# Sixty-six stores issued by GpSimd's queue instead of the sync engine's, in a hybrid attention and mLSTM step

## The chip, the cores and the metric

The kernel runs on one core of one Trainium2 chip, as one launch. The time is the device time of that core in microseconds (us). Five engines work side by side, each with an instruction queue of its own that it executes in order: PE (TensorE, matrix products; PEld is its weight load), DVE (VectorE), ACT (ScalarE), POOL (GpSimd) and SP (the sync engine, which here only issues DMAs). A DMA is issued by an instruction in the queue of one engine and is then carried out by the DMA engines; whoever needs its data waits for its semaphore. In the profile, "SPq", "ACTq" and "POOLq" are the queues, L729 is line 729 of the kernel, and a tile's name stands without its number.

## The reference, cut to what matters

One layer of a diffusion backbone, for 128 context tokens and 1024 latent tokens, all float32. Every matrix product is as wide as the model (1024) or the feed-forward part (2816).

```python
def trunk_layer(x, mods, ..., rope, ctx_kv, init_f, init_b):
    sh1, sc1, g1, sh2, sc2, g2 = mods            # silu(cond) @ w_ada + b_ada, six vectors
    h = rmsnorm(x, norm1_w) * (1 + sc1) + sh1
    aq, ak, av, mq, mk, mv, mo, mg = jnp.split(h @ w_in, SPLIT_POINTS, axis=-1)
    aq, ak = rmsnorm(aq, q_norm_w), rmsnorm(ak, k_norm_w)      # per head, 64 wide; then rotary
    attn_o = attention(aq, keys, vals)           # 8 query heads on 2 key/value heads
    hm, st_f, st_b = mlstm_bidir(heads(mq), heads(mk) * (MLSTM_DK ** -0.5), heads(mv),
                                 gates, init_f, init_b)        # 4 heads, two directions, chunks of 128
    hm = rmsnorm(hm, mlstm_norm_w) * sigmoid(mo)
    mix = jnp.concatenate([attn_o, hm], axis=-1) @ w_out
    x = x + g1 * mix
    h2 = rmsnorm(x, norm2_w) * (1 + sc2) + sh2
    x = x + g2 * swiglu(h2, w_gu, w_down)
    return x, ak, av, st_f, st_b
```

Returned are the normed outputs of both token groups and, of the context tokens, the keys and values, and the end states C, n and m of both scans of each head.

## The kernel before, in words

The 1152 tokens are nine blocks of 128 rows (block 0 is the context), grouped in three chunks of three blocks. float32 products are made of three PE passes on a rounded high part and the rest (`whi`, `wlo` of a weight, `hi` and `lo` parts of the data), the mLSTM's input products of scaled float16 pairs (`ipair`).

The stages, in order of time:

1. To about 135 us: the conditioning vectors from `w_ada`, the normed and turned tokens, and the projections of keys, values and gates. `k_work` (L688) norms and rotates the keys and stores the context's keys and values (L694, L695).
2. 115 to 195 us: `gate_work` (L535) computes the gates of all scans; it stores `new_state_m` (L617) and copies a three-part bfloat16 split of its maxima into a tile of another layout, SBUF to SBUF, with six DMAs (L648). Beside it `evac_q` (L716) norms and rotates the queries in groups of one or two blocks: POOL multiplies (L668, L685), DVE adds (L686), and each block goes to the DRAM tile `q_d` (L729), from which ACT's queue loads it again as `qr` (L999) for the attention.
3. 193 to 530 us: for each of four heads `head_project` (L743) makes queries, keys, values and output gates of nine blocks and updates the state of both directions block by block (`update`, L779: POOL forms `wv` in L783, PE multiplies in L785, DVE and ACT add to `cs`, L792 and L796). The end states of each head go to the outputs (L800, L801: two directions, two stores each). `head_mlstm` (L825) then reads the scans out, norms the result (L893, POOL) and stores a head's columns of `hm` into the DRAM tiles `hm_d` (L895), one store for each chunk of three blocks. `hm` has one buffer, so the next head's first write waits for these stores. Woven in are the first chunk's attention (`attention`, L991) and, at the end, the rest of the conditioning (`ada_rest`, L417), which takes its bias rows from DRAM (L448) and puts finished rows into the DRAM tile `g_d` (L454), and the first chunk's attention output (`attn_out_first`, L1205), which stores the sum as `x1a_d` (L1247).
4. 530 to 660 us: `prefill` (L1149) adds the mLSTM half of the output projection for all nine blocks: it loads `hm_d` (L1158) and `x1a_d` (L1163), and for the blocks of later chunks loads `x` (L1193), adds, and stores into `x1_d` (L1197).
5. 660 to 1590 us: the feed-forward part, chunk by chunk, in groups of four or five blocks of 128 hidden columns: `gate_up` (L1316), `down` (L1339), and `finish` (L1351), which norms the previous chunk and stores it to `y` (L1363). The last chunk ends in `down_last` (L1366), whose stores stand on ACT's and SP's queues (L1402, L1403).

Weights come through `load_piece` (L139, its DMA L151) and `ada_rest`'s L423 on SP, as do nearly all loads and the attention's transposing DMAs of the softmax's high and low parts (L1041, L1042). `dma` is `nc.sync.dma_start`.

What sets the order: the code yields between units of work and `weave` and `beside` mix these streams by given shares (`weave(head_project(0, sts[0]), beside((att, 0.1),), 96, 96)`). The tile framework then places each instruction in its engine's queue by a planner that plays the program through with durations of its own (`schedule_with_timeline_sim=True`); `hot(n)` raises the priority of a stretch. So an edit to one queue can also shift instructions on the other engines. The framework adds the semaphores: a store waits for its data, the next writer of a buffer for the store.

Of the kernel before, what the change touches and what calls it, by code (L numbers as in the profile page):

```python
# [19 lines left out]
P = 128  # L20
# [8 lines left out]
NH = 4  # L29
# [4 lines left out]
CB = 3  # L34
# [11 lines left out]
def hybrid_step(ctx: ExitStack, tc: tile.TileContext, I: dict, O: dict):  # L46
    nc = tc.nc
# [2 lines left out]
    dve = nc.vector  # L50
    pool = nc.gpsimd
    dma = nc.sync.dma_start
    uid = [0]

    def hot(n):
# [361 lines left out]
    def ada_rest(ns, silp, new_a4, new_part, new_row, early=2):  # L417


        def rows_of(n, j, q, half):  # L420
            a4 = new_a4()
            lo = n * D + j * 512 + q * 256
            dma(a4, w_ada[half * 512 : half * 512 + 512, lo : lo + 256].rearrange("(k p) n -> p k n", p=P))  # L423
            return a4

        units = [(n, j, q, half) for n in ns for j in range(2) for q in range(2) for half in range(2)]
        ahead = [rows_of(*u) for u in units[:early]]
        for u, (n, j, q, half) in enumerate(units):
            if u + early < len(units):
                ahead.append(rows_of(*units[u + early]))  # L430
            yield
            a4 = ahead.pop(0)
            if q == 0 and half == 0:
                ps = bank()
            for k in range(4):
                strip_products(ps[:, q * 256 : (q + 1) * 256], 4 * half + k, silp, a4[:, k, :])
            yield
            if q == 0 or half == 0:
                continue
            part = new_part()  # L440
            nc.scalar.copy(part, ps)
            yield
            if n in (3, 4):
                cols_from_strips(shift2 if n == 3 else scale2, n, j, part, bank)
                continue
            lo = n * D + j * 512
            row = new_row()
            dma(row, I["b_ada"][0:1, lo : lo + 512].to_broadcast([2, 512]))  # L448
            pr = bank()
            mm(pr[0:2, :], strip_sel, part, start=True, stop=True)  # L450
            dve.tensor_tensor(out=row, in0=pr[0:2, :], in1=row, op=ALU.add)
            if n == 5:
                dve.tensor_scalar(out=row, in0=row, scalar1=0.5, scalar2=None, op0=ALU.mult)
            dma(g_d[0 if n == 2 else 1, :, j * 512 : (j + 1) * 512], row)  # L454
        yield

    es_r = ExitStack()
# [77 lines left out]
    def gate_work(mlp):  # L535
# [57 lines left out]
        sm = g1("sm", rows=1)  # L593
# [3 lines left out]
        def blk(t, d, lo, hi):  # L597
            return t[:, d * 64 + 4 * lo : d * 64 + 4 * hi]
# [15 lines left out]
        dve.tensor_copy(blk(Mp, 1, 8, 9), m0[:, 4:8])  # L614
        dve.tensor_copy(blk(Mp, 1, 1, 8), blk(sm, 1, 2, 9))
        for d in range(2):
            dma(O["new_state_m"][0, 0, d : d + 1, :], blk(sm, d, 0, 1))  # L617
        dec = g1("dec", rows=1)
        dve.tensor_tensor(out=dec, in0=Mp, in1=Me, op=ALU.subtract)
        act(dec, dec, AF.Exp)  # L620
# [24 lines left out]
        dve.tensor_tensor(out=parts[2], in0=NM, in1=parts[1], op=ALU.subtract)  # L645
        for i in range(3):
            for d in range(2):
                dma(NM3[36 * i : 36 * i + 36, d, :], parts[i][64 * d : 64 * d + 36, :])  # L648
        for _ in range(6):
            yield  # L650
        ps = bank()
# [36 lines left out]
    def k_work(qp, cc, ss, kw):  # L688
        norm_rope(qp, cc, ss, kall[:, 9:10], 1, NKV, kw, (0, 0))
        yield  # L690
        for b in (0, 4):
            norm_rope(qp, cc, ss, kall[:, b : b + 4], 4, NKV, kw, (b, b + 4))
            yield
        dma(O["new_cache_k"][0, 0], kall[:, 9])  # L694
        dma(O["new_cache_v"][0, 0], vall[:, 9])  # L695

        vm = qp.tile([P, 4], F32, name="vm")
        dve.tensor_reduce(out=vm[:, 0:1], in_=vall, axis=AX.XYZ, op=ALU.max, apply_absolute_value=True)
        for _ in range(3):
            yield  # L700
        ps = bank()
        transpose(ps[0:1, 0:P], vm[:, 0:1])
        v1 = qp.tile([1, 4], F32, name="v1")
        dve.tensor_reduce(out=v1[:, 0:1], in_=ps[0:1, 0:P], axis=AX.X, op=ALU.max)
        dve.tensor_scalar(out=v1[:, 0:1], in0=v1[:, 0:1], scalar1=2.0 ** -80, scalar2=None, op0=ALU.max)
        dve.tensor_scalar(out=v1[:, 1:2].bitcast(I32), in0=v1[:, 0:1].bitcast(I32), scalar1=0x7F800000, scalar2=None, op0=ALU.bitwise_and)
        dve.tensor_scalar(out=v1[:, 2:3].bitcast(I32), in0=v1[:, 1:2].bitcast(I32), scalar1=-1, scalar2=268 * 2 ** 23, op0=ALU.mult, op1=ALU.add)
        dve.tensor_scalar(out=v1[:, 3:4], in0=v1[:, 1:2], scalar1=2.0 ** -28, scalar2=None, op0=ALU.mult)
        for _ in range(4):
            yield  # L710
        ps = bank()
        mm(ps[:, 0:2], one1, v1[:, 2:4], start=True, stop=True)
        dve.tensor_copy(vsc[:, 0:2], ps[:, 0:2])
        yield

    def evac_q(qp, cc, ss, qw):  # L716
        held = {}

        def evac(b, ps):
            grp = next(g for g in PAIRS if b in g)  # L720
            if b == grp[0]:
                held["t"] = qp.tile([P, 2, NQ, HD], F32, name=nm("qraw"), tag="qraw", bufs=2)
            qr = held["t"]
            act(qr[:, b - grp[0]], ps.rearrange("p (h d) -> p h d", d=HD), AF.Copy, scale=groups_in[0].inv)
            if b == grp[-1]:
                nb = len(grp)
                norm_rope(qp, cc, ss, qr[:, 0:nb], nb, NQ, qw, (max(grp[0], 1) - 1, grp[-1]))
                for i, bb in enumerate(grp):
                    dma(q_d[bb], qr[:, i].rearrange("p h d -> p (h d)"))  # L729

        return evac

# [10 lines left out]
    def head_project(h, st):  # L743
# [35 lines left out]
        def update(b, kt, va):  # L779

            wv = mlp.tile([P, 2, P + 1], F32, name=nm("wv"), tag="wv", bufs=2)
            for d in range(2):
                pool.tensor_tensor(out=wv[:, d], in0=va, in1=qcol(1, d, b, h).to_broadcast([P, P + 1]), op=ALU.mult)  # L783
            pc = bank()
            mm(pc[:, 0 : 2 * (P + 1)], kt, wv.rearrange("p d x -> p (d x)"), start=True, stop=True)  # L785
            for d in range(2):
                if b == (NBL if d == 0 else 1):
                    continue
                add = pc[:, d * (P + 1) : (d + 1) * (P + 1)]
                cn = mlp.tile([P, P + 1], F32, name=nm("cs"), tag="cs", bufs=CSB)  # L790
                if d == 0 and b > 0:
                    dve.scalar_tensor_tensor(out=cn, in0=states[0, b], scalar=decb[:, b * 4 + h : b * 4 + h + 1], in1=add,  # L792
                                             op0=ALU.mult, op1=ALU.add)
                    states[0, b + 1] = cn
                    continue
                nc.scalar.copy(cn, add)  # L796
                if b > 0:
                    raws[b] = cn
                    continue
                dma(O["new_state_C"][0, 0, d, h], cn[:, 0:P])  # L800
                dma(O["new_state_n"][0, 0, d, h].rearrange("(p o) -> p o", o=1), cn[:, P : P + 1])  # L801

        def q_group(cs):
            banks = [bankA() for _ in cs]
# [20 lines left out]
    def head_mlstm(h, st):  # L825
# [27 lines left out]
        for b in range(NB):  # L853
# [34 lines left out]
            if b in ends:  # L888
                b0 = ends[b]
                n = b + 1 - b0  # L890
                v = hm[:, b0 : b + 1, :]
                r = rsqrt(mlp, ssh[:, b0 : b + 1], n, 1.0 / P)
                pool.tensor_tensor(out=v, in0=v, in1=bc(r, 2, [P, n, P]), op=ALU.mult)  # L893
                for c in range(b0 // CB, b // CB + 1):
                    (nc.scalar.dma_start if h == NH - 1 and c > 0 else dma)(hm_d[c][:, h * P : (h + 1) * P].rearrange("(b p) n -> p b n", p=P), hm[:, c * CB : (c + 1) * CB, :])  # L895
            yield


# [250 lines left out]
    def prefill(cur, nxt):  # L1149
# [22 lines left out]
        for b in range(NB):  # L1172
# [12 lines left out]
            for n in range(2):  # L1185
                cs = slice(n * 512, (n + 1) * 512)
                ps = out_block(ws, n, th, tl)
                g = gx[n] if b == 0 else gs[n]
                if c < 2:
                    add_gated(x1s[c][i], ps, g, n, pool)  # L1190
                else:
                    xt = t2()
                    dma(xt, xrow(b)[:, cs])  # L1193
                    t = t2()
                    dve.tensor_tensor(out=t, in0=ps, in1=g, op=ALU.mult)
                    pool.tensor_tensor(out=xt, in0=xt, in1=t, op=ALU.add)
                    dma(x1_d[i][:, cs], xt)  # L1197
                yield
            if c == 0:
                with hot(200):  # L1200
# [4 lines left out]
    def attn_out_first(oT, ready):  # L1205
# [16 lines left out]
        def out():  # L1222
            for n in range(2):
# [8 lines left out]
                for i in range(CB):  # L1232
# [11 lines left out]
                    pool.tensor_tensor(out=v, in0=v, in1=gt[:, 4], op=ALU.add)  # L1244
                    yield
                    if n == 1:
                        dma(x1a_d[i], x1[:, i])  # L1247

        return out(), ada

# [100 lines left out]
    def finish(c, a):  # L1351
# [6 lines left out]
        for i in range(CB):  # L1358
            r = rs[i]
            for n in range(2):  # L1360
                v = x1[i][:, n * 512 : (n + 1) * 512]
                dve.scalar_tensor_tensor(out=v, in0=v, scalar=r, in1=fw[n], op0=ALU.mult, op1=ALU.mult)
            dma(yrow(c * CB + i), x1[i])  # L1363
            yield

    def down_last(c, a, f0, nf):  # L1366
# [178 lines left out]
```

## Time and profile before

| | us |
|---|---|
| three runs | 1586.22, 1588.04, 1590.58 |
| median | 1588.04 |
| profiled execution, span | 1590.3 |
| PE busy | 1494.7 (94%) |
| DVE busy | 1027.2 (65%) |
| ACT busy | 768.8 (48%) |
| POOL busy | 267.4 (17%) |

The profiled execution is given by its span, 1590.3 us, from its first instruction to its last; there is no separate time for it, and it lies inside the range of the three runs. An engine's busy time leaves out the issuing of DMAs, so SP has none. Idle time of an engine matters only where the engine that is waited for in the end, mostly PE, stands still because of it: the chain of waits tells which that is, and the table by stretches of 40 us tells where PE stands still. A row of the time line reads: start, duration, engine, line, operation, output and inputs, and in brackets how long the engine had been idle before it and what released it. A row of a list of waits reads: who waited, for what, the sum in us, how many times, and the longest.

### The profile page before, as it was taken

What the parts mean: (1) busy time and instruction counts of PE and PEld (TensorE: products, weight loads), DVE (VectorE), ACT (ScalarE), POOL (GpSimd) and SP (SyncE); (2) the same over time, 40 slices, a digit from 0 to 9 for tenths busy, and PEclk for the clock granted to TensorE, in tenths of its full rate; (3) what the DMA queues carried; (4) which work ended last, traced back from release to release, by engine and by line L of the source; (5) the groups of instructions that cost most, each with busy time, mean ns of one, the idle gap of its engine ahead of it and who ended that gap; (6) DMA issues with size and microseconds to landing.
All of it is one profiled execution on the core that took longest, in us unless ns stands there. A gap on an engine that the chain in (4) does not pass through costs nothing.

```text
span 1590.3 us, 23425 instructions
## 1 busy us (share of the span) xinstructions
PE 1494.7 (94%) x8539; PEld 1249.4 (79%) x8539; DVE 1027.2 (65%) x2025; ACT 768.8 (48%) x1409; POOL 267.4 (17%) x357
## 2 busy tenths in 40 slices
PE   6799799999988679999999999999999999999996
PEld 3544467666766467888999999999898989999995
DVE  4778645755757576667654667877875575554555
ACT  4854365846656354535433435555552443323332
POOL 0023342332332243100110001000010101001111
PEclk9899899999999899999999999999999999999998
DMA  9474322432547746957754547968774445544441
GB/s 358 160 200 140 94 75 36 103 77 52 117 113 179 237 103 149 221 158 176 173 158 129 159 127 230 198 154 198 165 173 126 153 133 178 155 121 137 146 144 53
DMA packets 387881, 236.91 MB, mean 149 GB/s; under 512 B 170198, under 2 KB 346790, under 8 KB 387766
## 3 DMA queue, kind: packets, MB, share of 16 engines
q1 hardware_dynamic: 385110, 231.84, 54.0%
q10 hardware_dynamic: 2656, 3.58, 1.1%
q8 instruction: 67, 1.10, 0.3%
q14 instruction: 48, 0.39, 0.1%
HBM read 183.79 MB, written 13.26 MB: 124 GB/s over the span
## 4 chain that ended last, share of the span: by engine, by line
PE 75%; DVE 9%; DMA 8%; ACT 4%; issue 2%; SPq 1%; POOL 1%; ACTq 0%; DVEq 0%; POOLq 0%
PE mm L1313 11%; PE mm L1314 11%; PE mm L1312 11%; PE mm L1112 5%; PE mm L1113 5%; PE mm L1114 5%; PE S L1032 4%; PE wi L485 3%; PE wi L483 3%; PE wi L484 3%; PE mm L1144 1%; PE mm L1145 1%; DMA aw<-in_w_ada_dram 1%; PE po L1057 1%; PE po L1056 1%
## 5 line engine op out<-in xcount | busy, mean ns | idle before, releaser
L152 ACT CAST whi<-raw 128x1024 fp32r<-128x1024 f32 (+1 forms) x216 | 221.8, 1027 | 413.0 <-PE mm L1313 151.5
L137 DVE TENSOR_TENSOR wlo<-raw,whi 128x1024 fp32r<-128x1024 f32 (+1 forms) x216 | 260.5, 1206 | 203.8 <-ACT whi L152 203.2
L1313 PE MATMUL mm<-aTl,whi 128*128 128x384 f32 x1056 | 355.9, 337 | 2.7 <-DVE aTl L137 2.7
L1314 PE MATMUL mm<-aTh,wlo 128*128 128x384 f32 x1056 | 354.3, 335 | 0.0
L1312 PE MATMUL mm<-aTh,whi 128*128 128x384 f32 x1056 | 353.2, 336 | 0.0
L137 POOL TENSOR_TENSOR hl<-tn,hl 128x384 fp32r<-128x384 f32 x66 | 85.5, 1295 | 839.5 <-ACT hl L1335 721.3
L1313 PEld LDWEIGHTS mm<-aTl,whi 128*128 128x128 f32 x1056 | 198.5, 188 | 3.9 <-DVE aTl L137 3.3
L1312 PEld LDWEIGHTS mm<-aTh,whi 128*128 128x128 f32 x1056 | 198.1, 188 | 0.6
L1314 PEld LDWEIGHTS mm<-aTh,wlo 128*128 128x128 f32 x1056 | 198.4, 188 | 0.0
L1113 PE MATMUL mm<-wlo,hl 128*128 128x512 f32 x372 | 145.5, 392 | 0.0
L1112 PE MATMUL mm<-whi,hl 128*128 128x512 f32 x372 | 144.1, 392 | 0.0
L1114 PE MATMUL mm<-whi,hl 128*128 128x512 f32 x372 | 143.2, 392 | 0.0
L483 PE MATMUL wi<-ipair,hT 128*128 128x384 f16 (+2 forms) x408 | 136.2, 337 | 1.8 <-ACT hT L507 1.2
L484 PE MATMUL wi<-ipair,hT 128*128 128x384 f16 (+2 forms) x408 | 136.4, 337 | 0.0
L485 PE MATMUL wi<-ipair,hT 128*128 128x384 f16 (+2 forms) x408 | 132.5, 337 | 1.0 <-DVE hT L137 1.0
L1039 DVE SCALAR_TENSOR_TENSOR pl<-pr,st,ph 128x1152 f16<-128x1152 f32 (+1 forms) x72 | 93.8, 1303 | 33.8 <-ACT ph L1038 33.7
L1034 DVE TENSOR_REDUCE st<-S 128x1 f32<-128x1152 f32 (+1 forms) x72 | 88.9, 1235 | 14.6 <-PE S L1032 14.1
L1032 PE MATMUL S<-kst,qT 128*128 128x384 f32 (+1 forms) x400 | 87.6, 350 | 9.8 <-ACT pr L1035 5.6
L1035 ACT ACTIVATE pr<-S,st 128x1152 f32<-128x1152 f32 (+1 forms) x72 | 81.3, 1129 | 29.6 <-DVE st L1034 25.6
L1038 ACT ACTIVATE ph<-pr,st 128x1152 f16<-128x1152 f32 (+1 forms) x72 | 83.8, 1165 | 23.2 <-DVE st L1037 6.7
L1101 DVE TENSOR_TENSOR t<-mm,gl 128x512 f32<-128x512 f32 x102 | 68.9, 685 | 28.1 <-DMA gl<-g_d 10.2
L1032 PEld LDWEIGHTS S<-kst,qT 128*128 128x128 f32 x400 | 70.6, 191 | 14.7 <-ACT pr L1035 7.0
(366 smaller groups left out, 2539.7 us busy)
## 6 DMA issues: line engine op xcount, KB each, us to landing
raw<-in_w_gu_dram SPq DMA_DIRECT2D x132, 512.0 KB
raw<-in_w_down_dram SPq DMA_DIRECT2D x60, 512.0 KB
a<-in_w_ada_dram SPq DMA_DIRECT2D x24, 512.0 KB
gl<-g_d SPq DMA_DIRECT2D x36, 256.0 KB
aw<-in_w_ada_dram SPq DMA_DIRECT2D x16, 512.0 KB
iraw<-in_w_in_dram SPq DMA_DIRECT2D x32, 256.0 KB
raw<-in_w_out_dram SPq DMA_DIRECT2D x12, 512.0 KB
x<-in_x_sample_dram SPq DMA_DIRECT2D x11, 512.0 KB
```

Source lines behind the costliest of these rows:

```text
L137: (dve if eng == "dve" else pool).tensor_tensor(out=out, in0=full, in1=hi, op=ALU.subtract)
L152: nc.scalar.copy(hi[:, :n], raw[:, :n])
L483: mm(ps[:, :n], ah, wh[:, k % 2, c0 : c0 + n], start=(k == 0), stop=False)
L484: mm(ps[:, :n], ah, wl[:, k % 2, c0 : c0 + n], start=False, stop=False)
L485: mm(ps[:, :n], al, wh[:, k % 2, c0 : c0 + n], start=False, stop=(k == KD - 1))
L1032: mm(S[:, n, 0:w], qT[:, h, :], kst[kv][:, t, c0 + n * w : c0 + (n + 1) * w], start=(t == 0), stop=(t == 1))
L1112: mm(ps, ah, wh[:, k % 2, :], start=(k == 0), stop=False)
L1113: mm(ps, ah, wl[:, k % 2, :], start=False, stop=False)
L1114: mm(ps, al, wh[:, k % 2, :], start=False, stop=(k == nk - 1))
L1312: mm(ps, wh[:, k, :], th[:, k, :], start=(k == 0), stop=False)
L1313: mm(ps, wh[:, k, :], tl[:, k, :], start=False, stop=False)
L1314: mm(ps, wl[:, k, :], th[:, k, :], start=False, stop=(k == KD - 1))
```

## The change

A second name, `put`, stands for GpSimd's `dma_start`. The stores that write a computed result to DRAM, and the six copies of L648, are issued through it. What is stored, where to, and all arithmetic stay. Sixty-six DMAs move: four of L454, two of L617, six of L648, one each of L694 and L695, nine of L729, eight each of L800 and L801, twelve of L895 (ten from SP and two from ACT's queue), six of L1197, three of L1247 and six of L1363. The last chunk's `y` stores and all loads stay where they were. The planner's order on the other engines shifts locally: on PE by some 50 places at most, among 10366.

```diff
     dma = nc.sync.dma_start
+    put = nc.gpsimd.dma_start
...
-            dma(g_d[0 if n == 2 else 1, :, j * 512 : (j + 1) * 512], row)
+            put(g_d[0 if n == 2 else 1, :, j * 512 : (j + 1) * 512], row)
...
-            dma(O["new_state_m"][0, 0, d : d + 1, :], blk(sm, d, 0, 1))
+            put(O["new_state_m"][0, 0, d : d + 1, :], blk(sm, d, 0, 1))
...
-                dma(NM3[36 * i : 36 * i + 36, d, :], parts[i][64 * d : 64 * d + 36, :])
+                put(NM3[36 * i : 36 * i + 36, d, :], parts[i][64 * d : 64 * d + 36, :])
...
-        dma(O["new_cache_k"][0, 0], kall[:, 9])
-        dma(O["new_cache_v"][0, 0], vall[:, 9])
+        put(O["new_cache_k"][0, 0], kall[:, 9])
+        put(O["new_cache_v"][0, 0], vall[:, 9])
...
-                    dma(q_d[bb], qr[:, i].rearrange("p h d -> p (h d)"))
+                    put(q_d[bb], qr[:, i].rearrange("p h d -> p (h d)"))
...
-                dma(O["new_state_C"][0, 0, d, h], cn[:, 0:P])
-                dma(O["new_state_n"][0, 0, d, h].rearrange("(p o) -> p o", o=1), cn[:, P : P + 1])
+                put(O["new_state_C"][0, 0, d, h], cn[:, 0:P])
+                put(O["new_state_n"][0, 0, d, h].rearrange("(p o) -> p o", o=1), cn[:, P : P + 1])
...
-                    (nc.scalar.dma_start if h == NH - 1 and c > 0 else dma)(hm_d[c][:, h * P : (h + 1) * P].rearrange("(b p) n -> p b n", p=P), hm[:, c * CB : (c + 1) * CB, :])
+                    put(hm_d[c][:, h * P : (h + 1) * P].rearrange("(b p) n -> p b n", p=P), hm[:, c * CB : (c + 1) * CB, :])
...
-                    dma(x1_d[i][:, cs], xt)
+                    put(x1_d[i][:, cs], xt)
...
-                        dma(x1a_d[i], x1[:, i])
+                        put(x1a_d[i], x1[:, i])
...
-            dma(yrow(c * CB + i), x1[i])
+            put(yrow(c * CB + i), x1[i])
```

## The prediction

> **What bounds the kernel now.** I read the page's shares and its chain of waits first, then the busy time by stretches of 40 us, then the waits of PE and of the sync engine's queue, and last the time line of the places where a moved store stands near an idle PE.
>
> ```profile
> span 1590.3 us, 23425 instructions
> PE 1494.7 (94%) x8539; PEld 1249.4 (79%) x8539; DVE 1027.2 (65%) x2025; ACT 768.8 (48%) x1409; POOL 267.4 (17%) x357
> PE 75%; DVE 9%; DMA 8%; ACT 4%; issue 2%; SPq 1%; POOL 1%; ACTq 0%; DVEq 0%; POOLq 0%
> ```
>
> PE is busy 94% of the span, and the queue of SP is 1% of the chain. So what the stores cost SP is not the prize; the 95.6 us in which PE is idle (1590.3 − 1494.7) are all that there is to win. The stretches (columns: start and end, length, then PE, PEld, DVE, ACT, POOL busy) show where they lie:
>
> ```profile
> 160.00:200.00 40.00, 30.79 (x158) 18.70 (x159) 24.87 (x65) 15.98 (x36) 13.53 (x13) 0.83 0.30 93
> 200.00:240.00 40.00, 40.00 (x255) 26.85 (x254) 18.05 (x60) 26.65 (x81) 15.24 (x38) 1.00 0.29 76
> 640.00:680.00 40.00, 37.73 (x224) 34.04 (x223) 28.98 (x38) 23.83 (x32) 4.23 (x4) 1.00 0.89 212
> 960.00:1000.00 40.00, 40.00 (x225) 38.82 (x224) 29.89 (x47) 19.23 (x28) 5.99 (x4) 1.00 0.77 240
> ```
>
> At 960, in the feed-forward part, PE has no idle time, though a batch of y stores stands in SP's queue there; a wait of SP that ends there moves nothing. Nearly all the idle time that a store could touch lies ahead of 680 us. The waits of SP at the moved stores (queue, line, what it waited for, total, times, longest) against its largest one:
>
> ```profile
> SPq L151 <- DVE wlo L137: 472.8, 171, 9.4
> SPq L729 <- DVE qraw L686: 32.4, 4, 12.4
> SPq L695 <- ACT vall L493: 13.2, 1, 13.2
> SPq L1247 <- POOL x1a L1244: 13.2, 3, 6.1
> SPq L800 <- ACT cs L796: 11.9, 1, 11.9
> SPq L1363 <- DVE x L1362: 10.2, 6, 3.9
> SPq L1197 <- POOL t L1196: 6.4, 4, 4.1
> ```
>
> These six, 87.3 us of waiting, leave SP. But a weight load (L151) waits for its buffer 472.8 us all the same, so SP mostly trades one wait for another.
>
> **The change part by part.** Sixty-six stores go to POOL's queue, 64 from SP's and two (the last head's hm_d) from ACT's. No arithmetic is added. POOL executes in order, so each store stands between its arithmetic, and a store that waits holds what follows. PE's order changes only locally.
>
> No trace here shows a store issued by POOL. Its price in POOL's queue is bounded below by the cheapest issue on SP, 0.25 us, and above by a whole small store from issue to landing, 173.66 to 175.75, 2.09 us, as if POOL stood until the data was there. I take 1.0 us, nearest to the six stores of L648 (5.68 / 6 = 0.95):
>
> ```profile
> 155.53 2.41 POOL L685 TENSOR_TENSOR qraw<-qraw,cc 128x1024 f32<-128x1024 f32 x1 [1.82 <-DVE nr L679]
> 155.75 5.68 SPq L648 DMA_DIRECT2D NM<-nmp  x6
> 158.12 0.23 DVE L644 CAST nmp<-NM 128x128 bf16<-128x128 f32 x1
> 160.92 1.22 DVE L686 TENSOR_TENSOR qraw<-qraw,nr 128x1024 f32<-128x1024 f32 x1
> 162.64 0.92 SPq L729 DMA_DIRECT2D q_d<-qraw  x2
> 167.16 1.27 ACT L724 ACTIVATE qraw<-wi,isc 128x512 f32<-128x512 f32 x2 [0.92 <-DMA q_d<-qraw]
> 167.90 1.12 PE L116 MATMUL mm<-ident,qr 128*128 128x128 f32 x4 [1.55 <-ACT qraw L724]
> 173.66 0.34 SPq L729 DMA_DIRECT2D q_d<-qraw  x1
> 175.77 0.69 ACT L724 ACTIVATE qraw<-wi,isc 128x512 f32<-128x512 f32 x1 [1.05 <-DMA q_d<-qraw]
> 529.89 0.25 SPq L454 DMA_DIRECT2D g_d<-ir  x1
> ```
>
> Front, 150 to 180: the rows are the chain that I follow. In the changed order four of the six L648 stores stand ahead of POOL's L685. The second pair needs the cast at 158.12, ready at 158.35; with two issues of 1.0 L685 starts at 160.35, ends at 162.76, and DVE's L686 starts there, not at 160.92: +1.8 us. L686 ends at 163.98; the last two L648 hold POOL until 164.76; the two q_d stores take 2.0, not 0.92, and end at 166.76, not 163.56: +3.2 at the queries that PE transposes at 167.90. The second q_d store (173.66) feeds ACT's next L724 and through it the following PE gap; it gets the 1.8 and 0.7 of issue, while ACT no longer stands 0.92 in front of its L198 work, because the changed order puts the two L724 behind it: +1.6 to +2.5. PE is full from 200 on, so what is lost here stays lost. I take +2; with 0.25 an issue it is 0, below it −1 because the iraw loads no longer stand behind L648 on SP; with 2.09 it is about +6.
>
> [...]
>
> Heads, 195 to 490: 16 stores of the end states (L800, L801) in bursts of four and the hm_d stores in groups.
>
> ```profile
> 203.75 0.85 POOL L783 TENSOR_TENSOR wv<-va,QT 128x129 f32<-128x129 f32 x2 [2.07 <-ACT va L757]
> 261.64 0.75 POOL L783 TENSOR_TENSOR wv<-va,QT 128x129 f32<-128x129 f32 x2 [3.70 <-ACT va L757]
> 344.83 0.10 POOL L758 MEMSET va<- 128x1 f32 x1 [2.99 <-PE mm L870]
> 424.12 0.75 POOL L783 TENSOR_TENSOR wv<-va,QT 128x129 f32<-128x129 f32 x2 [3.51 <-ACT va L757]
> 428.51 0.86 POOL L783 TENSOR_TENSOR wv<-va,QT 128x129 f32<-128x129 f32 x2 [2.65 <-ACT va L757]
> PE wi L808 <- ACT th L760: 2.1, 1, 2.1
> ```
>
> POOL's idle gap next to each of the four bursts is 2.07, 3.70, 2.99 and 3.51, in all 12.3 us, or 0.77 per store. At 1.0 the bursts overflow by 16 − 12.3 = 3.7 us, and a following gap such as the 2.65 takes that up; wv (L783) comes late by that much and PE needs it at L785. The two hm_d stores that leave ACT give it back two issues, at a place where PE waits for nothing of ACT's queue: 0. I take +1, from 0 (at 0.25) to +13 (16 × 2.09 = 33.4, less 12.3 and less four gaps of 2). Nothing is queued on SP behind these stores but transposes that wait for their own operands: SP's gain is 0, and no more than PE's idle time there. The changed order also puts PE's L785 12 to 28 places later in the first blocks of two heads, which the trace does not price; I take +1.5, near the one wait of PE on this stream's gates, 2.1, with −2.1 and +4.2 as ends.
>
> At 476 to 488 a whole head's hm waits for three stores before its buffer (there is one) is written again:
>
> ```profile
> 478.89 1.46 SPq L895 DMA_DIRECT2D hm_d<-hm  x3
> 479.83 4.37 DMA hm_d<-hm
> 487.70 0.49 PE L840 MATMUL mm<-qT,kT 128*128 128x128 f32 x2 [1.05 <-ACT it L866]
> 509.80 0.64 PE L341 MATMUL mm<-ip,gta 128*32 128x256 f32 x8 [1.41 <-DMA ip<-in_w_ada_dram]
> 520.91 8.24 SPq L1247 DMA_DIRECT2D x1a_d<-x1a  x3
> 531.55 1.29 SPq L1041 DMA_TRANSPOSE phT<-ph  x1
> 541.48 1.11 PE L116 MATMUL mm<-ident,t 128*128 128x128 f32 x4 [6.44 <-DMA t<-hm_d]
> ```
>
> Three issues of 1.0 against 1.46 in all are +1.5, of which I take +1 at PE (0 to +4.8). At 498 to 511 SP is spared a g_d store and a row load goes behind the two ip loads: their gap of 1.41 at 509.80 goes, −1.4 (0 to −2.1, with the second gap of the same load). At 520.91 to 530.14 SP is spared three x1a_d stores and a g_d store, but the next in its order are the transposes, which waited until 531.55 for PE; the loads for t<-hm_d come after them, so the gap of 6.44 stays: 0.
>
> Start of the feed-forward part, 607 to 665:
>
> ```profile
> 617.25 4.69 DMA t<-in_x_sample_dram
> 626.32 0.50 PE L1144 MATMUL mm<-whi,mx 128*128 128x512 f32 x1 [1.24 <-DVE t L1195]
> 628.18 0.50 PE L1146 MATMUL mm<-whi,mx 128*128 128x512 f32 x1 [1.13 <-DVE mx L137]
> ```
>
> The x_d stores stood on SP among the t loads and two transposes; in the changed order the load at 617.25 goes ahead of these, some 4 us earlier. That clears the two gaps: −2.4. The stretch of 640 holds another 2.27 us of PE idle, behind weight loads which SP issues sooner; I leave it, because the t buffers come free by the stores' landing, now 0.7 later (ends −4.6 and +1.4).
>
> Feed-forward, 680 to 1560, and the end: the six y stores are spared SP, PE is full, and POOL is idle for long stretches: 0. If that cover were gone, six issues of 1.0 would cost 6. The last stage's y stores aren't moved. The two state_m and two cache stores on POOL free SP of the 13.2 us of L695, but the loads next to them wait for PE's use of their buffers: 0 (to −0.5).
>
> Sum: +2 + 1 + 1.5 + 1 − 1.4 − 2.4 = +1.7 us. On the profiled span that is 1592.0. The span shown, 1590.3, is 2.3 above the median of the three runs, 1588.04, and nearly the slowest of them, 1590.58; on the median the forecast is 1589.7, rounded 1590.
>
> **The rivals.**
> Slower, POOL's queue becomes the bound of the heads: a store costs POOL about 2 us. It decides from 0.77 us on, where the four bursts no longer fit. At 1.8, halfway up, 16 × 1.8 = 28.8, less 12.3 and 8, is +8.5; with the front (+5) and hm (+4) against −3.8 of gains that gives +14, 1602. For it speaks that POOL is the only queue of arithmetic here which had issued no DMA; against it that POOL is idle 83% of the span. [...]
>
> Slower, the front alone: the issue costs 1.0 as taken, but the +3.2 passes whole to both PE gaps, and the gain at 626 fails, as SP's loads wait for buffers anyway: 3.2 + 2.5 + 1 + 1.5 + 1 − 1.4 = +7.8, 1596. For it: 472.8 us of waits of L151.
>
> Faster: SP is free from 514 on, PE reaches its own transposes' operands earlier, and the gap of 6.44 goes with the 4.6 us of 620 to 665 and 1.4 at 509, while stores cost POOL 0.25 and the front stays: −6 to −12, at its middle 1579. For it: 8.24 us of x1a_d stores right ahead; against it the order of SP.
>
> No change that matters: an issue on POOL costs 0.25 to 0.45 as on SP, the front and the heads lose nothing, and 509 and 626 give −3.8: 1584 to 1588.
>
> **How the numbers follow.** 0.3%, 4.8 us, is about what a measurement of this kernel can tell from no change: the three runs lie 0.28% apart. My forecast gets 0.30 (its own range 1586 to 1594), the cheap store 0.12, the bound in the heads 0.25, the front alone 0.15, faster 0.18. So within 0.3% is 0.42, slower 0.40, faster 0.18. The range, 1582 to 1606, reaches into the faster case from below, where about 0.1 is left out, and beyond the 1602 of the heads' case, where another 0.1 is.
>
> **What would show it.** The profile after should have rows of POOL's queue for L648, L729, L800 and L895 near 1.0 us each. PE's gap at 167.90 and the next one should grow by 2 to 3 us in all. The gaps at 509.80, 626.32 and 628.18 should be gone; that of 6.44 should stay; the stretches from 680 on should stay at 40.00; the six waits of SP should be missing and L151's grow. Rows of 2 us in POOL's queue, or PE waits for wv in the heads, make me wrong upward; t<-hm_d issued before 530 downward.

## The result and the profile after

The changed kernel takes 1596.95 us (median of seven runs, 1592.99 to 1599.84), the kernel before 1588.8 us in the same count of runs. The ratio is 1.0052 with a 95% interval from 1.0035 to 1.0068: about 8 us slower (6 to 11). That lies inside the range of the prediction, 1582 to 1606, beyond its likeliest case (1586 to 1594), and on the side to which it gave 0.40.

In all profiles with a time of their own the time is the span plus 1.7 to 1.9 us (after: 1593.5 and 1591.7). By that measure the profiled execution of before, with its span of 1590.3, would be a time of some 1592, above the highest run of that kernel in any round (1591.6). So it does not lie inside the range of the runs, as was said beside the table of before. Where a profile of before is needed below I therefore also use that of the first experiment, `e2_y`, which moves only six hidden stores and takes the same time as before; where the two differ, both are given.

In the changed kernel all lines from 53 on stand one higher: L730 is what was L729. Lines of its page (shares, queues, groups of section 5 and of the view by lines):

```profile
span 1591.7 us, 23465 instructions
PE 1494.0 (94%) x8539; PEld 1251.3 (79%) x8539; DVE 1026.7 (65%) x2025; ACT 771.6 (48%) x1409; POOL 305.6 (19%) x423
q0 software_dynamic: 4224, 11.75, 2.1%
L730 POOL DMA_DIRECT2D q_d<-qraw x9 | 5.2, 574 | 5.4 <-DVE qraw L687 3.6 <-DVE shift L334 1.5 <-POOL qraw L671 0.3
L649 POOL DMA_DIRECT2D NM<-nmp x6 | 3.1, 528 | 1.1 <-DVE nmp L643 1.1
L896 POOL DMA_DIRECT2D hm_d<-hm x12 | 9.4, 788 | 1.5 <-POOL hm L894 1.5
```

The 66 stores are there, as 66 more instructions of POOL (357 to 423), in a DMA queue of another kind. POOL's busy time does count them, unlike SP's: it grows by 38.2 us. A store occupies POOL for 0.53 to 0.79 us by the means of these groups: dearer than the 0.25 to 0.45 of most of SP's issues before, cheaper than the 1.0 that I took. The state stores, 0.54 to 0.57 each, are below the 0.77 that fit into POOL's gaps.

What PE waited for (engine, line, what; us in total, times, longest), and SP at its largest wait:

```profile
PE mm L117 <- ACT qraw L725: 8.2, 1, 8.2
PE S L1033 <- ACT pr L1036: 8.1, 3, 4.6
PE mm L117 <- DMA t<-hm_d: 4.5, 2, 4.2
PE mm L342 <- DMA ip<-in_w_ada_dram: 1.2, 2, 0.7
SPq L152 <- DVE wlo L138: 480.6, 178, 9.5
```

The wait for t<-hm_d shrank from 6.4 to 4.5, that for ip from 2.1 to 1.2, and of the two gaps at 626 and 628 only 0.2 us is left. Two took their place: 8.2 us for ACT's L725 (1.5 before) and one of 4.6 for L1036 (the longest of these was 2.1 before). The busy time of the engines by stages, first of `e2_y`, then of the changed kernel (start and end, length, PE, PEld, DVE, ACT, POOL busy; the third number from the right is the granted clock):

```profile
130.00:190.00 60.00, 49.38 (x281) 26.64 (x280) 48.67 (x115) 28.14 (x51) 18.59 (x11) 0.86 0.38 120
460.00:530.00 70.00, 57.72 (x355) 43.24 (x353) 56.10 (x150) 40.06 (x106) 25.43 (x30) 0.95 0.56 150
530.00:600.00 70.00, 50.41 (x254) 38.60 (x254) 45.12 (x104) 30.24 (x49) 23.30 (x18) 0.95 0.62 180
600.00:700.00 100.00, 96.12 (x529) 83.95 (x529) 66.90 (x92) 47.48 (x61) 14.76 (x11) 1.00 0.74 188
```

```profile
130.00:190.00 60.00, 45.14 (x260) 23.22 (x259) 47.32 (x122) 27.69 (x51) 27.58 (x25) 0.86 0.37 112
460.00:530.00 70.00, 58.59 (x374) 43.97 (x372) 55.41 (x145) 41.09 (x107) 29.77 (x40) 0.98 0.57 150
530.00:600.00 70.00, 52.56 (x240) 40.02 (x238) 46.28 (x111) 30.87 (x51) 24.63 (x22) 0.85 0.63 185
600.00:700.00 100.00, 95.20 (x521) 82.64 (x520) 64.89 (x92) 45.64 (x58) 20.85 (x19) 0.98 0.72 179
```

Against `e2_y`, PE idles 4.2 us more in the front (10.6 to 14.9), and gains and losses of 0.9 to 2.2 us follow. In the stretch from 530 PE is busier by 2.15 us and yet finishes fewer products (240 against 254): its clock there is 0.85 and not 0.95. I had summed only idle time; this is the second half of the account, and I come back to it. Two profiles of kernels that take the same time differ too, though: in before's own, PE's idle time in the four stretches is 11.3, 12.8, 19.2 and 4.6 us, and in the third the clock is 0.90 and PE finishes 243 products. Against that one the front has 3.6 us more, and the last stretch 0.2.

The front, in the rows of the changed kernel, step by step:

```profile
156.35 2.09 POOL L649 DMA_DIRECT2D NM<-nmp  x4 [1.10 <-DVE nmp L643]
158.45 4.35 POOL L686 TENSOR_TENSOR qraw<-qraw,cc 128x1024 f32<-128x1024 f32 x1
160.57 3.32 DVE L220 SCALAR_TENSOR_TENSOR ipair<-iraw,isc,ipair 128x1024 f16<-128x1024 f32 x1
163.81 1.21 DVE L687 TENSOR_TENSOR qraw<-qraw,nr 128x1024 f32<-128x1024 f32 x1
165.32 1.12 POOL L730 DMA_DIRECT2D q_d<-qraw  x2 [1.52 <-DVE shift L334]
171.13 0.63 ACT L199 ACTIVATE jkw<-iraw 128x512 bf16<-128x512 f32 x1 [2.73 <-DMA iraw<-in_w_in_dram]
172.52 1.25 ACT L725 ACTIVATE qraw<-wi,isc 128x512 f32<-128x512 f32 x2
173.24 1.11 PE L117 MATMUL mm<-ident,qr 128*128 128x128 f32 x4 [8.19 <-ACT qraw L725]
```

The four copies are ahead of POOL's multiply as the order said, and the q_d stores end at 166.44; I had 166.76. Then ACT's L725, which turns the next queries out, stands behind passes over the next weights (L199), one of which waits 2.73 us for its load. PE's wait for it grew by 6.6 us. Against that, the one just ahead of it shrank by 2.9: PE waited 3.83 us for `part` before (L347) and waits 0.90 now (L348).

### The profile page after: what moved, and what is told of

Its sections match the earlier page's. It is cut to its first block, busy times and chain, and to the rows that moved or that the text cites. A ratio compares the mean times of both kernels' runs of the same rounds, so it can differ in the third digit from the quotient of the medians.

```text
span 1591.7 us, 23465 instructions
## 1 busy us (share of the span) xinstructions
PE 1494.0 (94%) x8539; PEld 1251.3 (79%) x8539; DVE 1026.7 (65%) x2025; ACT 771.6 (48%) x1409; POOL 305.6 (19%) x423
## 4 chain that ended last, share of the span: by engine, by line
PE 70%; DVE 5%; ACT 3%; DMA 2%; issue 1%; SPq 0%; ACTq 0%; DVEq 0%
PE mm L1314 11%; PE mm L1315 11%; PE mm L1313 11%; PE mm L1113 5%; PE mm L1114 5%; PE mm L1115 5%; PE S L1033 4%; PE mm L1145 2%; PE mm L1146 2%; PE mm L1147 2%; PE po L1058 1%; PE po L1057 1%; PE wi L484 1%; PE wi L486 1%; PE wi L485 1%
## 5 line engine op out<-in xcount | busy, mean ns | idle before, releaser
L1033 PE MATMUL S<-kst,qT 128*128 128x384 f32 (+1 forms) x400 | 88.8, 354 | 11.3 <-ACT pr L1036 8.1
L1035 DVE TENSOR_REDUCE st<-S 128x1 f32<-128x1152 f32 (+1 forms) x72 | 88.9, 1234 | 14.4 <-PE S L1033 14.1
L1036 ACT ACTIVATE pr<-S,st 128x1152 f32<-128x1152 f32 (+1 forms) x72 | 81.5, 1132 | 28.8 <-DVE st L1035 24.7
L1102 DVE TENSOR_TENSOR t<-mm,gl 128x512 f32<-128x512 f32 x102 | 69.2, 688 | 27.8 <-DMA gl<-g_d 12.8
```

The source lines that it names most:

```text
L1033: mm(S[:, n, 0:w], qT[:, h, :], kst[kv][:, t, c0 + n * w : c0 + (n + 1) * w], start=(t == 0), stop=(t == 1))
```

## The experiments

Each is the kernel before with some stores moved to POOL (`put`), timed in turn with the kernel before; `e12_after_order` and `e17_all_but_qd` start from the changed kernel instead, and `e10_qd_act` moves its stores to ACT. Line numbers are those of before. First the parts.

**Only the y stores** (`e2_y`):

```diff
-            dma(yrow(c * CB + i), x1[i])
+            put(yrow(c * CB + i), x1[i])
```

> Only the six y stores of L1363 go to POOL's queue, at places where PE has no idle time. The theory of places (a moved store costs only where PE then waits): 0, within 2 us of before. A fixed cost of having a queue of GpSimd at all: the whole difference of the change, some +8 us. A cost spread evenly over the 66 stores (8.2 / 66 = 0.12 us each): +0.7.

Measured: 0.9993 (0.9980 to 1.0006), −1 us (−3 to +1). A queue of GpSimd costs nothing that could be told by being there, nor do six stores where PE is full.

**Only the front** (`e3_front`: L648, L729):

```diff
-                dma(NM3[36 * i : 36 * i + 36, d, :], parts[i][64 * d : 64 * d + 36, :])
+                put(NM3[36 * i : 36 * i + 36, d, :], parts[i][64 * d : 64 * d + 36, :])
...
-                    dma(q_d[bb], qr[:, i].rearrange("p h d -> p (h d)"))
+                    put(q_d[bb], qr[:, i].rearrange("p h d -> p (h d)"))
```

> Only the fifteen stores of L648 and L729 go to POOL. The theory of places: the idle time of PE between 158 and 184 us grows from 9.5 to 12 us or so, the time by +2.5 to +5. Spread evenly: +1.9. Heads theory (the cost of the change lies in the heads): 0 to +1.

Measured: 1.0071 (1.0048 to 1.0093), +11 us: more than the whole change. So a place that I had not seen was in it. Rows of this kernel, ACT and PE at 209 us, and the views of the tile q_d and of line L801 (last lines):

```profile
208.52 0.37 ACT L1035 ACTIVATE pr<-S,st 128x128 f32<-128x128 f32 x1 [9.25 <-DMA q_d<-qraw]
209.03 0.69 PE L1032 MATMUL S<-kst,qT 128*128 128x128 f32 x2 [5.79 <-ACT pr L1035]
DMA to landing us min/median/max: 2.3/2.6/9.2
DMA to landing us min/median/max: 9.2/9.2/9.2
```

The last q_d store, issued at 199.24, landed 9.2 us later. ACT's first softmax tile waits 9.25 us for the last q_d stores, presumably because it takes over the memory of the query tiles. A store of the state n (L801), 128 pieces of 4 bytes, took 9.2 us to land here, and SP now sends two of them and the C stores at 199 to 201, no longer behind the q_d stores but beside them.

**Only the heads** (`e4_heads`: L800, L801, L895, as in the change):

> Only the 28 stores of L800, L801 and L895 go to POOL. The rival that POOL's queue is the bound of the heads: +6 to +10, with PE waiting for wv or th. The theory of places with the 0.57 us per store that the profile of the change shows, under the 0.77 that fit into POOL's gaps: 0 to +3. Spread evenly: +3.5.

Measured: 1.0002 (0.9991 to 1.0013). That is −1 to +2 us, for 28 stores; the rival that POOL's queue becomes the bound of the heads had +6 to +10, and is out.

**Only the late stores** (`e5_late`: L454, L1197, L1247, as in the change):

> Only the thirteen stores of L454, L1197 and L1247 go to POOL. The theory of places: a gain, -2 to -6 us, from the loads that SP issues sooner between 498 and 665 us. Spread evenly: +1.6. If SP's waits were all hidden: 0.

Measured: 1.0014 (1.0003 to 1.0026), +2 us: no gain but a small loss, against what I expected. Two of the gaps that I meant to close did close, and another opened (rows of this kernel, ACT and PE):

```profile
636.51 1.05 ACT L152 CAST whi<-raw 128x1024 fp32r<-128x1024 f32 x1 [7.50 <-DMA raw<-in_w_gu_dram]
640.19 1.22 ACT L1035 ACTIVATE pr<-S,st 128x1152 f32<-128x1152 f32 x1
641.55 1.68 PE L1032 MATMUL S<-kst,qT 128*128 128x384 f32 x6 [4.08 <-ACT pr L1035]
```

The planner now puts ACT's softmax tile behind two casts of feed-forward weights, where in `e2_y` it stood behind one. The first cast waits for its load and starts no sooner than there (636.51, 635.70 in `e2_y`), and PE waits 4.08 us in one piece. The changed kernel has the same wait (4.56).

**Only L648** (`e8_nm`) and **only L729** (`e9_q`), the two halves of the front:

> Only the six copies of L648 go to POOL. Fifteen stores of the front cost +11 us (L648 and L729 together). Theory A (the planner puts ACT's absolute-value passes over the next weights, L198, ahead of the L724 that feed PE, and on the chip L198 stands waiting for its loads): three of them stand ahead here, against one before and five with all fifteen: +1 to +4. Theory B (the landing of the last q_d store, behind the state stores that SP sends at the same time): these stay on SP, so 0. Theory C (every copy on POOL delays the rotary multiplies L685): +2 to +3 from L648 alone.

> Only the nine stores of L729 go to POOL. Theory B: most of the 11 us is here, +6 to +9, with ACT's L1035 waiting for the last q_d store at about 200 us and PE for ACT. Theory A: three L198 stand ahead of the L724, +1 to +4. Theory C: 0 to +1.

Measured: L648 1.0003 (0.9989 to 1.0018); L729 1.0058 (1.0042 to 1.0074), +9 us. The copies that I had put at the root of the front's loss cost nothing by themselves; the q_d stores cost it. But `e8_nm` doesn't try the step that I had predicted, because the planner gives the copies another place there. In the change four of them stand ahead of POOL's multiply; here all six stand behind it, and it takes its 2.41 us as before:

```profile
152.19 2.41 POOL L685 TENSOR_TENSOR qraw<-qraw,cc 128x1024 f32<-128x1024 f32 x1 [1.83 <-DVE nr L679]
154.55 3.21 POOL L648 DMA_DIRECT2D NM<-nmp  x6
```

The same holds for `e3_front` and `e13_front_cn`. And the +9 of `e9_q` is not theory B: there the longest landing of a q_d store is 5.1 us, no wait stands at 203 us, and +9 remains.

**The state stores behind the q_d stores** (`e13_front_cn`: L648, L729, L800, L801):

> The fifteen front stores and the sixteen state stores of L800 and L801 on POOL, so that the state stores stand behind the last q_d stores in one queue and don't pass them. Theory B: the wait of ACT's L1035 for the last q_d store falls from 9.2 to 3 us, and the time from +11 to about +6. Theory A alone: +11 stays.

**The first head's n stores left out** (`e18_front_no_n0`):

```diff
-                dma(O["new_state_n"][0, 0, d, h].rearrange("(p o) -> p o", o=1), cn[:, P : P + 1])
+                if h > 0: dma(O["new_state_n"][0, 0, d, h].rearrange("(p o) -> p o", o=1), cn[:, P : P + 1])
```

> The fifteen front stores on POOL, and the two stores of the first head's state n (128 pieces of 4 bytes each) are left out, so that new_state_n lacks head 0; everything else is computed. If those pieces hold up the last q_d store in the DMA engines: it lands in 2.6 us, not 9.2, the wait of PE at 203 us goes, and the time falls from +11 to +5 or +6, like with the state stores behind it in POOL's queue. If the state C stores or the queue itself hold it up: 9 us and +11 stay.

Measured: for `e13_front_cn` 1.0039 (1.0025 to 1.0052), +6 us, and for `e18_front_no_n0` 1.0030 (1.0016 to 1.0044), +5 us, each some 5 to 6 us less than the front alone. Without the two n stores the q_d stores of `e18_front_no_n0` land in 2.6 us by their median and in 4.5 at most, ACT waits 1.0 us for the last of them and not 9.25, and PE, which waited 5.79 us from 203 in `e3_front`, is busy throughout from 200 to 220. By itself that is not clean: in `e18_front_no_n0` SP also issues the C stores later, from 202.13, after both q_d stores and not beside them. The changed kernel has the cleaner case. There the four state stores of head 0 stand in one queue, C, n, C, n. The first C store has nothing small ahead of it, the second stands right behind an n store; the two last lines are their times to landing:

```profile
205.46 0.58 POOL L801 DMA_DIRECT2D out_new_state_C_dram<-cs  x1
206.03 0.54 POOL L802 DMA_DIRECT2D out_new_state_n_dram<-cs  x1
206.56 0.54 POOL L801 DMA_DIRECT2D out_new_state_C_dram<-cs  x1
DMA to landing us min/median/max: 1.8/1.8/1.8
DMA to landing us min/median/max: 10.0/10.0/10.0
```

So in these two kernels a store near the 4-byte pieces landed 7 to 8 us later: in 9.2 against a median of 2.6 in `e3_front`, and in 10.0 against 1.8 here. About half of `e3_front`'s +11 goes with this wait. The change itself moves both and doesn't have this wait: ACT waits 3.03 us for the last q_d store there, and 3.21 did before.

**The q_d stores on ACT's queue** (`e10_qd_act`):

```diff
-    dma = nc.sync.dma_start
+    dma = nc.sync.dma_start; put = nc.scalar.dma_start
...
-                    dma(q_d[bb], qr[:, i].rearrange("p h d -> p (h d)"))
+                    put(q_d[bb], qr[:, i].rearrange("p h d -> p (h d)"))
```

> Only the nine q_d stores move, to ACT's queue and not to POOL's. If it is leaving SP's queue that costs, since the order against SP's loads and state stores is lost: +5 to +10, as on POOL. If it is POOL's queue (the store behind and among POOL's arithmetic, the issue of 0.57 us): 0 to +3. ACT's queue is held at each store until DVE's L686 is done, which could cost ACT's work behind it some 2 us at five places.

Measured: 1.0063 (1.0045 to 1.0081), +10 us, as much as on POOL in `e9_q`, and with the wait for the landing that `e3_front` has:

```profile
210.71 0.37 ACT L1035 ACTIVATE pr<-S,st 128x128 f32<-128x128 f32 x1 [8.13 <-DMA q_d<-qraw]
211.22 0.69 PE L1032 MATMUL S<-kst,qT 128*128 128x128 f32 x2 [5.28 <-ACT pr L1035]
```

So that wait is not tied to GpSimd's queue (8.13 us of ACT's L1035 here, 9.25 in `e3_front`): in these runs it came where a q_d store was issued beside the state stores (here at 200.47, SP's at 198.63 to 199.98) and no longer ahead of them in SP's. It doesn't show that the nine stores cost +9 and +10 for the same reason. In `e9_q` the last q_d store is issued at 201.17, ahead of the state stores (from 202.67), the wait is missing, and the loss is as large.

**ACT's order forced** (`e11_front_order` on the front, `e12_after_order` on the change in full):

```diff
-            act(qr[:, b - grp[0]], ps..., AF.Copy, scale=groups_in[0].inv)
+            act(qr[:, b - grp[0]], ps..., AF.Copy, scale=groups_in[0].inv); b == 6 and nc.scalar.copy(jkw[:, 0:1], qr[:, b - grp[0], 0, 0:1])
```

> All fifteen front stores on POOL, as before, and one column of the queries copied by ACT into the tile that L198 writes, after block 6: that forces L724 ahead of all L198 in ACT's queue. One copy of 128x1 is added, no result changes. Theory A: the idle time of PE between 158 and 180 us falls by 3 us or so, and the time from +11 to +7 or +8; if A carried all of it, to 0. Theory B: the wait at about 203 us stays, 4 to 6 us. If neither: +11 as with the fifteen stores alone.

> The change in full, with the one-column copy that forces ACT's L724 ahead of L198. In the changed kernel PE waits 8.2 us for L724 at 165 to 173. If the order in ACT's queue made that wait: it falls to 2 or 3 us, and the time from +8 to +3 or +4. If L724 then waits as long for its buffer, that is for the landing of the q_d stores: +8 stays.

Measured: 1.0102 (1.0084 to 1.0119), +16 us, and 1.0050 (1.0034 to 1.0067), +8 us. Theory A falls as an account of the time. In the change, L724 now runs as soon as its buffer is free, and PE's wait is still 6.30 us, for the store's landing:

```profile
167.27 1.26 ACT L724 ACTIVATE qraw<-wi,isc 128x512 f32<-128x512 f32 x2 [3.71 <-DMA q_d<-qraw]
168.01 1.11 PE L116 MATMUL mm<-ident,qr 128*128 128x128 f32 x4 [6.30 <-ACT qraw L724]
```

Forcing the order took 1.9 us off the 8.19, no more, and the time did not follow even that. On the front alone PE reached the first state update earlier (194.7 against 198.2 us), and then waited 7.46 us for the last q_d store, which landed 10.5 us after its issue.

**All but the q_d stores** (`e17_all_but_qd`: the change with L729 left on SP):

> The change without its nine q_d stores: these stay on SP, the other 57 go to POOL. If the q_d stores carry the loss (they alone cost +9, the six copies of L648 nothing): 0 to +3, the rest being the late stores' +2. In ACT's queue the L198 passes still stand ahead of L724 here; if that order by itself were the cost: +5 to +8, with PE's wait of some 8 us at 165 to 173 still there.

Measured: 1.0045 (1.0026 to 1.0064), +7 us. I can't reduce this result to the parts as they were moved. The q_d stores cost +9 alone, and without them the other 57 cost +7, though the y, head and late stores and L648 give, each alone, −1, 0, +2 and 0. The stores of L617, L694 and L695 were moved in no experiment of their own. Its profile does show two places. It has the change's order in the front, four copies ahead of the multiply, and with the q_d stores on SP PE still waits 5.06 us for L724 (first three lines); and the late wait has grown to 6.23 us (last two):

```profile
157.45 4.36 POOL L685 TENSOR_TENSOR qraw<-qraw,cc 128x1024 f32<-128x1024 f32 x1
159.59 3.31 DVE L219 SCALAR_TENSOR_TENSOR ipair<-iraw,isc,ipair 128x1024 f16<-128x1024 f32 x1
169.17 1.11 PE L116 MATMUL mm<-ident,qr 128*128 128x128 f32 x4 [5.06 <-ACT qraw L724]
644.73 1.04 ACT L152 CAST whi<-raw 128x1024 fp32r<-128x1024 f32 x1 [9.43 <-DMA raw<-in_w_gu_dram]
650.00 2.29 PE L1032 MATMUL S<-kst,qT 128*128 128x384 f32 x6 [6.23 <-ACT pr L1035]
```

PE's idle time from 130 to 190 us is 13.2 us there and from 600 to 700 it is 6.5, against 11.3 and 4.6 in the profile of before and 10.6 and 3.9 in `e2_y`: 4 to 5 us in these two places. The copies and the late stores are the same as in `e8_nm` and `e5_late`; what differs is the order that the planner makes of them together.

## Where the time went

The idle time of PE (span less busy time) doesn't follow the time. `e9_q` has 93.5 us of it, `e2_y` 93.1, and the spans differ by 7.3. What differs is PE's busy time, for the same 8539 products, and the mean granted clock. Page and clock of `e2_y`, then of `e9_q`:

```profile
PE 1492.4 (94%) x8539; PEld 1248.3 (79%) x8539; DVE 1027.0 (65%) x2025; ACT 768.6 (48%) x1409; POOL 269.2 (17%) x363
core 0: 1585.5 us, clock 0.978
```

```profile
PE 1499.3 (94%) x8539; PEld 1253.8 (79%) x8539; DVE 1029.9 (65%) x2025; ACT 768.7 (48%) x1409; POOL 272.0 (17%) x366
core 0: 1592.8 us, clock 0.972
```

In the clock records of the profiles of before and after the granted clock is 1.0 or 0.5. A stretch at 0.5 lasts 3.41, 6.83 or 10.24 us in both, and 13.65 once after, but for the last stretch of a profile; the stretches at 1.0 between them are multiples of 3.41 too (75.09, 22 times, before). What happens at one gap, in four successive steps of 3.41 us of the changed kernel:

```profile
132.57:135.98 3.41, 2.80 (x32) 1.52 (x31) 3.41 (x8) 0.00 (x0) 3.19 (x4) 1.00 0.37 102
135.98:139.39 3.41, 1.47 (x8) 0.77 (x9) 3.20 (x10) 2.54 (x5) 2.19 (x2) 1.00 0.70 210
139.39:142.81 3.42, 3.42 (x11) 1.47 (x9) 3.31 (x9) 3.35 (x6) 2.88 (x4) 0.51 0.57 184
142.81:146.22 3.41, 3.41 (x22) 1.32 (x21) 3.32 (x6) 2.83 (x6) 1.21 (x2) 0.99 0.48 150
```

PE is busy 1.47 us of the second step, 43%; in the third it is busy throughout at half the clock and finishes 11 products, against 22 in the fourth. I take the gap of 2.55 us in the second step (PE's wait for DVE's L334 at 137.92) to have cost another 1.7, half of the 3.41 that follow. That the gap brought on the half clock is an inference from this order in time; no experiment here varies a gap alone.

So the account has two terms: idle time, and half of the time in which PE was busy at the half clock, added up from those records. With both taken off the span, the rest is 1466 to 1471 us in the seven profiles below. So the two terms account for the differences to within 5 us. The losses to be explained are 5 to 16 us, so a third term of some us may be missing:

| kernel | span | idle | lost to the half clock | rest |
|---|---|---|---|---|
| before | 1590.3 | 95.6 | 23.9 | 1470.8 |
| `e2_y` | 1585.5 | 93.1 | 23.6 | 1468.9 |
| after | 1591.7 | 97.7 | 27.6 | 1466.4 |
| `e9_q` | 1592.8 | 93.5 | 32.9 | 1466.4 |
| `e13_front_cn` | 1593.3 | 93.3 | 34.3 | 1465.8 |
| `e3_front` | 1599.1 | 102.9 | 28.0 | 1468.2 |
| `e17_all_but_qd` | 1593.5 | 99.7 | 26.8 | 1466.9 |

Against `e2_y`, the changed kernel's profile has 4.6 us more idle time and 4.0 us more lost to the clock, less 2.5 in the rest: +6.2. Against before's own profile it is 2.1 and 3.7, less 4.4: +1.4. One profile to a kernel is thin ground for such a sum. The edges of the steps lie elsewhere in each profile (1.9, 2.6, 2.9 and 3.3 us behind a multiple of 3.41 from the first instruction in `e17_all_but_qd`, before, after and `e3_front`), so the same gap may fall into one step or across two.

The mean clock, though, is on record for every timed run. It is 0.9775 to 0.9777 on average for the kernel before, in three rounds of 22 to 29 runs, 0.9747 for the changed kernel (seven runs), and 0.9748, 0.9745 and 0.9742 for `e3_front`, `e9_q` and `e10_qd_act`; the runs of one kernel scatter by 0.002. In the changed kernel's profile a clock of 0.975 goes with 27.6 us lost, 1.1 us for each 0.001. By this estimate the clock carries some 3 us of the change's 8, and 3 to 4 of `e9_q`'s 9. The 9.3 by which `e9_q` exceeds `e2_y` in the table is more than that because the profile of `e9_q` fell on the run with the lowest clock of its six (0.972). The other 5 to 6 us of `e9_q` stay open. In its profile PE waits 5.75 us for L724 at 171.10 and idles 15.3 us from 130 to 190, 4 to 5 more than before and `e2_y`, but from 530 to 600 it idles 3.5 to 3.9 us less (15.7), so the sum hides the front.

## Why the prediction was right or wrong

Right: the range, which reached far enough up, and 0.40 for slower, with the front named as a place of the loss. Of the two slower rivals "the front alone", +7.8 and 1596, comes closest, in size and in its main step; the failing gain at 626 was part of it too. Its size is in part luck: 3.5 of its 7.8 us stand for the heads, the reorder and hm_d, which moved alone (`e4_heads`) cost −1 to +2, and it has nothing for the clock, some 3 us. The top of the range was set by the rival of the heads, which did not happen. Wrong: the likeliest case, whose sum of +1.7 came out as +8. The steps that failed are the front behind the q_d stores, the late gain, and a wait's price without the half clock.

- *The price of a store on POOL, 1.0.* It was 0.53 to 0.79. Too high, and it hardly mattered: y and heads, 34 stores, cost nothing that could be told. (PE's and DVE's queues had issued no DMA before either, so POOL's was not "the only queue of arithmetic" of that kind.)
- *The front, +2.* The step held up to the q_d stores (issue ended 166.44; predicted 166.76), by two errors that cancel: the issues were cheaper, and POOL's multiply took 4.35 us for 2.41, while DVE's L220 ran beside it and took 3.32 for 1.28. The pair comes back with this order, 4.35 and 3.31 in `e12_after_order`, 4.36 and 3.31 in `e17_all_but_qd`; and before, DVE's small L643 took 2.26 us beside POOL's multiply, and 0.29 in the change, where POOL had no multiply beside it. What lengthened them is not shown. After 166 the step failed. The query transposes came 5.3 us later than before (173.24 against 167.90), not 3.2, as ACT ran its weight passes first; with these forced behind (`e12_after_order`) PE still waited, for the landing of the q_d stores. Of PE's idle time in the stretch +3.6 to +4.2 stayed, not +2: this is the term that was mis-sized.
- *Which store of the front.* I derived the loss from L648 ahead of the multiply. L648 alone costs 0, L729 alone +9. Neither tries that chain: in both, no copy stands ahead of the multiply in POOL's queue. The profiles have it only where the change is moved whole or nearly so (`e12_after_order`, `e17_all_but_qd`), and there the copies do delay the multiply.
- *The reorder, +1.5 with ends of −2.1 and +4.2.* It stood for PE's L785 in the heads. From 190 to 460 us PE's idle time is 7.1 us in the change and 5.9 before, +1.1, and 5.4 in `e4_heads`: about as taken, or nothing. What the sum lacked was another reorder, of ACT at the late stores: L1036 behind two casts put 4.56 us in place of the gaps that were to go. In the stretch from 600 PE's idle time went from 3.9 (`e2_y`) or 4.6 (before) to 4.8, not down by 2.4.
- *The gains, −1.4 and −2.4.* The gaps for ip went from 1.41 and 0.69 to 0.55 and 0.69 in the changed kernel, 0.9 of the 1.4 that I took; those at 626 and 628 went and came back as one. `e5_late` has the sign: +2, not −3.8. I had said what is late next there (the t buffers) and named the wrong thing: it was the cast's load of weights.
- *The wait of 6.44 for t<-hm_d that stays.* It became 4.16, with 3.25 just ahead of it for DVE: 7.4 us in place of 7.7 for the two (1.30 and 6.44 before). It stayed.
- *A wait costs its length.* The sum counted idle time alone. It lacked the half clock: 4.0 us in this profile against `e2_y`, some 3 by the clocks of all runs.
- *The heads.* The rival gave POOL's stores 2 us. They took 0.79 at most on average, and the 28 of `e4_heads` cost −1 to +2 us in all.
- *The noise.* The three runs of before lie 0.27% apart, not 0.28%.

What stays open: why the q_d stores alone cost 9 us, and why the change without them still costs 7. The parts don't add, and each build has another order on PE, ACT and DVE; no experiment here holds every order fixed and changes the queue alone. So it is not shown how much of the 8 us is the queue's and how much the planner's.

## What to carry to other kernels

A store's queue is also its place in line: ask what the store was ahead of in its old queue, above all stores of tiny pieces (here 128 of 4 bytes, 9.2 us to land), before what it was waiting for. Where a planner orders the program, an edit to one queue is an edit to all of them, and parts measured alone need not add up to the whole. And where a trace shows the half clock after waits of PE, as here, price a wait by its length plus that: by my estimate up to 1.7 us for each 3.41 at half clock, 27.6 in all in the changed kernel's profile.

## What the runs showed of the hardware

- The granted clock after a step with idle time. I cut the profiles of before and after into steps of 3.41 us at the edges of their clock records and took the steps at full clock. Where PE was busy under 40% of a step, the next was at half clock in all 15 cases (7 before, 8 after), between 40% and 60% in 7 of 19, from 60% on in 2 of 845. The idle time came in several pieces too: before, waits of 0.96 and 0.60 us at 382 and 384 us, in a step in which PE was busy 54%, were followed by 3.41 us of half clock.
- A store of the state n, 128 pieces of 4 bytes, took 7.8 to 11.4 us to land (8.0 in `e12_after_order`, 9.2 in `e3_front`, 9.7 to 10.7 in the changed kernel, 7.8 to 11.4 in `e17_all_but_qd`). A q_d store, 256 KB, issued beside such stores from another queue took 9.2 us in `e3_front` and 10.5 in `e11_front_order`, from POOL's, against a median of 2.6 in each, and some 10 from ACT's in `e10_qd_act` (issue 200.47, ACT released at 210.71). In one queue, a store of 64 KB right behind such pieces took 10.0 us, the one ahead of them 1.8 (the changed kernel).
- A store of q_d issued by POOL landed 2.3 us after its issue at the shortest (the changed kernel), one from SP 2.1 (before: issue 173.66, landed 175.75): 0.2 later. Beside weight loads that SP issued, one of POOL's took 3.9 (the changed kernel: issue 165.88, SP's loads from 159.48 to 167.28), and one of SP's 3.92 (before: issue 163.13); the longest of POOL's in `e9_q` took 5.1.
- Beside POOL's multiply, DVE's L643, 128x128 with two inputs, took 2.26 us (before), and 0.29 where POOL had no arithmetic to do (the changed kernel). Why is not shown.
